# Mixer with a mixture of experts: 2 MB weight loads with 16 KB rows, and modulation on the tensor engine

## The chip, the cores and the metric

The kernel runs on one core of a Trainium2 chip, in FP32. The metric is the device time of one launch in microseconds (us). Three runs of the kernel before took 1287.95 to 1289.67 us, median 1289.12. The trace comes from one further, profiled execution of 1286.36 us. TensorE (PE) multiplies matrices, VectorE (DVE), ScalarE (ACT) and GpSimd (POOL) do the rest, and SyncE (SP) issues most of the loads. Each engine works through its own instructions in a fixed order.

## The reference

256 latent tokens and 256 context tokens of width 1024 go through one layer:

```python
sh1, sc1, g1, sh2, sc2, g2 = adaln(c, w_ada[l], b_ada[l])        # silu(c) @ w_ada + b_ada, 6 x 1024
csh1, csc1, cg1, csh2, csc2, cg2 = adaln(c_ctx, w_ada[l], b_ada[l])
pl = split_cols(modulate(rms_norm(x, norm1_g[l]), sh1, sc1) @ w_in[l])
pc = split_cols(modulate(rms_norm(ctx, norm1_g[l]), csh1, csc1) @ w_in[l])
yc_ml, yl_ml = mlstm_mixer(pc[:4], pl[:4], ...)                  # 4 heads, both directions
yc_hg, yl_hg = hgrn2_mixer(pc[4:], pl[4:], ...)                  # 4 heads, both directions
x = x + g1 * (jnp.concatenate([yl_ml, yl_hg], axis=-1) @ w_out[l])
hl2 = modulate(rms_norm(x, norm2_g[l]), sh2, sc2).reshape(bsz * seq, d)
x = x + g2 * moe_ffn(hl2, ...)                                   # top 4 of 32 experts, clamped SwiGLU
return rms_norm(x, final_g)
```

Only the first two of the six modulation vectors are wanted for the context. An expert has w_gu of 1024 x 2048 and w_down of 1024 x 1024, 12 MB; the 32 of them are 384 MB, w_in is 1024 x 4112 (all but the 16 gate columns is 16 MB), w_ada 24 MB, w_out 4 MB.

## The kernel before

**Weights.** Every large weight comes through one buffer, a ring of slots of 1 MB (8 KB in each of 128 partitions), filled by `load_rows` (L109 to L116) from SyncE's queue, in program order; a load is issued when its slot is free. The ring starts with 5 slots (`NR`) and grows by 8, 2 and 3 as the front's buffers are given up: 18 from the start of the experts on. A load of w_gu takes 128 rows of the matrix, one whole row of 8 KB to a partition. A load of w_down takes 256 rows, two rows of 4 KB to a partition, which are 128 rows apart. A load of w_in is a block of 256 columns (1 KB rows), one of w_ada or w_out 256 rows of 1024 columns.

**Splitting.** FP32 passes on TensorE are replaced in the front by fp32r passes on split numbers: `halves` (L82 to L89) makes wh, a rounded copy, on ScalarE (L87) and the rest wl on VectorE (L88). A product is then three passes (hh wh, hl wh, hh wl: L273 to L275, L290 to L292).

**The front.** The tokens come in (`xin`), are normalised and transposed into `hT`. The first 2048 columns of the modulation are 8 loads of w_ada, split, and 64 matmuls with the 4 columns of `silr` (L239, L240). Their sums `arow` are folded into columns by 16 tiny matmuls (L248), from which `mod` and `gain` come. Then `hm` = hT gain + mod, its rounded part `hh` (L325) and rest `hl` (L326) follow block by block. The gate projection takes 24 passes (L352 to L354) with the split small weight `wg`, which ScalarE's queue has loaded and VectorE split (L226, L227). The projections, the scans of the two head groups, the output gates and the output projection follow. The other 4096 columns of modulation, g1, sc2, sh2 and g2, are made beside the projections by 32 VectorE instructions (`gemv`, L586): each adds 128 rows of w_ada times `silc` to an accumulator `aacc`. `row` (L625) sums an accumulator over the partitions with two matmuls with ones, which leave the row in all partitions at once. The places of these instructions among the others are those of a scheduler that follows program order, with `issue_after` where one must not run early.

**The experts.** For a pair of experts `dispatch` gathers up to 64 tokens each, through one-hot matmuls (L923) into XT, one block of 128 features at a time. `expert` multiplies XT by 8 slots of w_gu (L941, in two groups of 64 columns that work side by side), evacuates the sum to `gu`, transposes it in 8 blocks of 128 (L950), applies the bias `bgT` and the SwiGLU, and multiplies by 4 slots of w_down (L974). `combine` adds the outputs (L986).

Of the kernel before, what the change touches and what calls it, by code (L numbers as in the profile page):

```python
# [9 lines left out]
FT = mybir.dt.float32  # L10
# [9 lines left out]
D = 1024  # L20
# [3 lines left out]
NR, NR2, NR3, NR4 = 5, 8, 2, 3  # L24
# [4 lines left out]
def tile_hybrid_backbone(  # L29
# [52 lines left out]
    def halves(src):  # L82

        wh = split.tile([128, 1024], FR, name="wh")
        wl = split.tile([128, 1024], FR, name="wl")
        with tc.high_priority(min(ahead, tc.cur_priority)):
            act(wh, src, AF.Copy)  # L87
            dve.tensor_sub(wl, src, wh.bitcast(FT))  # L88
        return wh, wl  # L89
# [36 lines left out]
    aacc = [fo.tile([128, D], FT, name=f"aacc{i}") for i in range(3)]  # L126
# [54 lines left out]


# [36 lines left out]
    wgh = px.tile([128, 8, 128], FR, name="wgh")  # L219
    wgl = px.tile([128, 8, 128], FR, name="wgl")  # L220
    nc.gpsimd.memset(wgh.bitcast(FT), 0.0)
    nc.gpsimd.memset(wgl.bitcast(FT), 0.0)
    wg4 = wg.rearrange("p a (g h) -> p a g h", g=4)
    wgh4 = wgh.rearrange("p a (g r) -> p a g r", g=4)[:, :, :, 0:4]
    wgl4 = wgl.rearrange("p a (g r) -> p a g r", g=4)[:, :, :, 0:4]
    dve.tensor_copy(wgh4, wg4)  # L226
    dve.tensor_sub(wgl4, wg4, wgh4.bitcast(FT))  # L227


    pa = [pj.tile([128, 512], FT, name="pj") for _ in range(4)]  # L230
    for g in range(2):
        for q in range(4):
            w = wa.pop(0) if wa else load_rows(w_ada[0], 256 * q, 2, g * D, D)
            for i in range(2):
                k = 2 * q + i
                wh, wl = halves(w[:, i])
                for n in range(2):
                    s = slice(n * 512, (n + 1) * 512)
                    mm(pa[2 * g + n][0:4, :], silr[:, k], wh[:, s], start=(k == 0), stop=False)  # L239
                    mm(pa[2 * g + n][0:4, :], silr[:, k], wl[:, s], start=False, stop=(k == 7))  # L240

    arow = px.tile([4, 2048], FT, name="arow")
    for n in range(4):
        (act(arow[:, n * 512:(n + 1) * 512], pa[n][0:4, :], AF.Copy) if n % 2 else
         dve.tensor_copy(arow[:, n * 512:(n + 1) * 512], pa[n][0:4, :]))
    pt = bank()
    for b in range(16):
        mm(pt[:, 2 * b:2 * b + 2], arow[:, b * 128:(b + 1) * 128], fold4, start=True, stop=True)  # L248
    mod = fc.tile([128, 16, 2], FT, name="mod")
    dve.tensor_tensor(mod, pt[:, 0:32].rearrange("p (b w) -> p b w", w=2),  # L250
                      cols[:, col["ba"]:col["ba"] + 16].unsqueeze(2).to_broadcast([128, 16, 2]), op=OP.add)
    gain = fc.tile([128, 8, 2], FT, name="gain")
    dve.scalar_tensor_tensor(gain, mod[:, 8:16], 1.0,
# [4 lines left out]
    def proj_split(w):  # L258

        return [halves(w[:, 4 * i:4 * i + 4, :].rearrange("p a f -> p (a f)")) for i in range(2)]  # L260

    def proj_cols(c0, t0s, parts=None):

        ps = [pj.tile([128, 512], FT, name="pj") for _ in t0s]
        w = None if parts else load_rows(w_in[0], 0, 8, c0, 256)
        for i in range(2):
            wh, wl = parts[i] if parts else halves(w[:, 4 * i:4 * i + 4, :].rearrange("p a f -> p (a f)"))
            for a in range(4):
                k = 4 * i + a
                for j, t0 in enumerate(t0s):  # L270
# [4 lines left out]
                    mm(o, wl[:, s], hh[:, k, t0:], start=False, stop=(k == 7))  # L275
        return ps

    def proj_tok(c0, tiles):

        ps = [pj.tile([128, 512], FT, name="pj") for _ in range(len(tiles) // 2)]  # L280
        w = load_rows(w_in[0], 0, 8, c0, 256)
        for i in range(2):
            wh, wl = halves(w[:, 4 * i:4 * i + 4, :].rearrange("p a f -> p (a f)"))
# [36 lines left out]
    first = proj_split(load_rows(w_in[0], 0, 8, 2576, 256))  # L320
    for k in range(8):
        hm = px.tile([128, 512], FT, name="hm", bufs=2)
# [108 lines left out]
    def hgrn_inputs(hp, parts=None):  # L431
# [10 lines left out]
        if hp == 0:  # L442
            gemv(2, aacc[0], last_hl)
            gemv(4, aacc[1], last_hl)
# [184 lines left out]
    for i in range(3):  # L629
        row(i, aacc[i])  # L630
# [479 lines left out]
```

## Time and profile before

| what | value |
|---|---|
| runs (3), median | 1289.12 us (1287.95 to 1289.67) |
| profiled execution, own time | 1286.36 us |
| its span, first to last instruction | 1284.3 us |
| mean granted TensorE clock | 0.982 |
| PE busy | 1164.2 us (91%) |
| DVE busy | 478.9 us (37%) |
| ACT busy | 267.7 us (21%) |
| HBM read | 453.69 MB, 354 GB/s over the span |
| share of the chain that ended last | PE 58%, DMA 34%, DVE 4% |

A busy PE isn't PE at its peak, and a share over the whole span is an average over stages with different limits. The slices of the span and the windows show each stage. The chain of waits is followed back from the last instruction; it names what released each step. MB are 10^6 bytes in the profile's rates and volumes; sizes of loads and slots are 1,048,576 bytes to the MB.

### The profile page before, as it was taken

Reading aid. Unit: us, or ns where it says so; the run is one execution under the profiler, and the core shown is the slowest. Engines: PE = TensorE matmul, PEld = TensorE weight load, DVE = VectorE, ACT = ScalarE, POOL = GpSimd, SP = SyncE. Lnnn points to the kernel's source line nnn. Section 1 sums busy time; section 2 is a strip of 40 time slices with the busy share of each in tenths; the row PEclk is TensorE's granted clock in tenths of the full one; section 3 lists DMA queues with packets and bytes.
Section 4 is the critical chain, followed back from the end, with each engine's and each line's share of the span. In section 5 each row is a group of like instructions: output and inputs, shape, how many; then the busy total and the mean of one; then the engine's idle time right before and its main releaser. Section 6 shows DMA issues by size and latency. Waiting matters only on the chain.

```text
span 1284.3 us, 14494 instructions
## 1 busy us (share of the span) xinstructions
PE 1164.2 (91%) x5708; PEld 562.0 (44%) x5709; DVE 478.9 (37%) x983; ACT 267.7 (21%) x492; POOL 108.2 (8%) x199
## 2 busy tenths in 40 slices
PE   4899999998999999889989988998899889979895
PEld 1578998896633343343323322432243234223221
DVE  7988999687121321312112221121211121112124
ACT  5666566563110000001000100100010001000001
POOL 5000000301301010110001100110020002000001
PEclk9889999998899999999999999999999999999998
DMA  9583533349899999999999999999999999999994
GB/s 332 200 295 129 180 101 126 118 171 419 323 393 416 417 418 415 402 417 416 416 417 417 417 417 417 417 417 417 416 416 417 417 417 415 417 416 417 417 415 174
DMA packets 99738, 455.77 MB, mean 355 GB/s; under 512 B 8809, under 2 KB 25282, under 8 KB 66896
## 3 DMA queue, kind: packets, MB, share of 16 engines
q1 hardware_dynamic: 97104, 452.62, 88.1%
q0 software_dynamic: 1200, 1.56, 0.4%
q8 instruction: 47, 0.77, 0.2%
q10 hardware_dynamic: 1360, 0.60, 0.2%
q14 instruction: 27, 0.22, 0.0%
HBM read 453.69 MB, written 1.05 MB: 354 GB/s over the span
## 4 chain that ended last, share of the span: by engine, by line
PE 58%; DMA 34%; DVE 4%; ACT 2%; issue 1%; POOL 0%; ACTq 0%; SPq 0%; DVEq 0%
PE pu L941 21%; DMA w<-w_gu_dram 19%; DMA w<-w_down_dram 14%; PE pd L974 9%; PE pm L923 5%; PE pm L986 3%; PE pj L275 2%; PE pj L273 2%; PE pj L274 2%; PE pt L950 1%; DMA wg<-w_in_dram 1%; PE pj L290 1%; PE pj L292 1%; PE pj L291 1%; DVE wl L88 1%; PE m L502 1%
## 5 line engine op out<-in xcount | busy, mean ns | idle before, releaser
L941 PE MATMUL pu<-w,XT 128*64 128x512 f32 x2048 | 467.9, 598 | 33.6 <-DMA w<-w_gu_dram 33.6
L941 PEld LDWEIGHTS pu<-w,XT 128*64 128x64 f32 x2048 | 136.4, 136 | 327.7 <-issue 229.2
L974 PE MATMUL pd<-w,aT 128*64 128x512 f32 x1024 | 240.5, 604 | 13.8 <-DMA w<-w_down_dram 12.3
L957 DVE TENSOR_TENSOR gl<-pt,bgT 128x512 f32<-128x512 f32 x32 | 22.1, 692 | 328.9 <-PE pt L950 328.9
L974 PEld LDWEIGHTS pd<-w,aT 128*64 128x64 f32 x1024 | 66.1, 137 | 150.3 <-issue 104.2
L76 ACT ACTIVATE gu<-pu 128x512 f32<-128x512 f32 x48 | 26.9, 595 | 493.0 <-PE pu L941 493.0
L78 DVE COPY gu<-pu 128x512 f32<-128x512 f32 x16 | 11.1, 692 | 270.5 <-ACT gu L76 270.5
L977 DVE TENSOR_TENSOR YP<-pd,g2b 64x512 f32<-64x512 f32 x64 | 44.0, 688 | 109.8 <-PE pd L974 109.1
L923 PEld LDWEIGHTS pm<-S,h 128*128 128x128 f32 x512 | 65.4, 202 | 39.3 <-issue 34.7
L914 POOL TENSOR_SCALAR S<-islot,posm 128x64 f32<-128x64 f32 x60 | 25.2, 443 | 675.2 <-PE pm L929 606.1
L923 PE MATMUL pm<-S,h 128*128 128x128 f32 x512 | 73.9, 294 | 2.2 <-DVE S L914 1.0
L986 PE MATMUL pm<-YP,GT 128*128 128x512 f32 x128 | 62.6, 614 | 11.0 <-DVE YP L977 11.0
L88 DVE TENSOR_TENSOR wl<-w,wh 128x1024 fp32r<-128x1024 f32 x55 | 66.6, 1218 | 6.0 <-ACT wh L87 5.7
L87 ACT ACTIVATE wh<-w 128x1024 fp32r<-128x1024 f32 x55 | 57.5, 1061 | 43.8 <-PE pj L274 22.1
L925 ACT ACTIVATE XT<-pm 128x512 f32<-128x512 f32 x32 | 19.0, 596 | 203.7 <-PE pm L923 203.7
L275 PE MATMUL pj<-hh,wl 128*128 128x512 f32 (+1 forms) x160 | 58.6, 371 | 3.0 <-DVE wl L88 3.0
L274 PE MATMUL pj<-hl,wh 128*128 128x512 f32 (+1 forms) x160 | 59.6, 373 | 0.0
L273 PE MATMUL pj<-hh,wh 128*128 128x512 f32 (+1 forms) x160 | 59.0, 374 | 0.2 <-ACT wh L87 0.2
L950 PE MATMUL pt<-ident,gu 128*128 128x128 f32 x256 | 39.3, 283 | 14.9 <-ACT gu L76 14.9
L950 PEld LDWEIGHTS pt<-ident,gu 128*128 128x128 f32 x256 | 27.3, 141 | 54.3 <-ACT gu L76 32.6
L960 ACT ACTIVATE sg<-gl 128x512 f32<-128x512 f32 x32 | 20.2, 630 | 142.5 <-DVE gl L958 142.5
L986 PEld LDWEIGHTS pm<-YP,GT 128*128 128x128 f32 x128 | 21.9, 189 | 50.2 <-issue 26.3
(455 smaller groups left out, 1236.6 us busy)
## 6 DMA issues: line engine op xcount, KB each, us to landing
w<-w_gu_dram SPq DMA_DIRECT2D x256, 1024.0 KB, 19.9
w<-w_down_dram SPq DMA_DIRECT2D x128, 1024.0 KB, 20.1
w<-w_ada_dram SPq DMA_DIRECT2D x24, 1024.0 KB, 6.2
w<-w_in_dram SPq DMA_DIRECT2D x16, 1024.0 KB, 5.8
w<-w_out_dram SPq DMA_DIRECT2D x4, 1024.0 KB, 5.0
xin<-x_dram SPq DMA_DIRECT2D x1, 1024.0 KB, 7.5
xin<-ctx_dram SPq DMA_DIRECT2D x1, 1024.0 KB, 12.3
x<-x_dram POOLq DMA_DIRECT2D x1, 1024.0 KB, 5.3
```

The source lines that it names most:

```text
L76: act(o, i, AF.Copy)
L87: act(wh, src, AF.Copy)
L88: dve.tensor_sub(wl, src, wh.bitcast(FT))
L273: mm(o, wh[:, s], hh[:, k, t0:], start=(k == 0), stop=False)
L274: mm(o, wh[:, s], hl[:, k, t0:], start=False, stop=False)
L275: mm(o, wl[:, s], hh[:, k, t0:], start=False, stop=(k == 7))
L923: mm(p_[:, i * ns:(i + 1) * ns], h2[:, a, (k + i) * 128:(k + i + 1) * 128], S[:, a, 0:nj].rearrange("p j s -> p (j s)"), start=(a == 0), s ...
L941: mm(ps[64 * j:64 * j + 64, n * 512:(n + 1) * 512], XT(k), w[:, 0, j * 1024 + n * 512:j * 1024 + (n + 1) * 512], start=(k == 0), stop=(k = ...
L950: nc.tensor.transpose(pt[:, f * 128:(f + 1) * 128], s[:, f * 128:(f + 1) * 128], ident)
L974: mm(pd_[64 * n:64 * n + 64, :], aT[:, k], w[:, i, n * 512:(n + 1) * 512], start=(k == 0), stop=(k == 7))
L977: dve.tensor_mul(yp[:, f], pd_[64 * n:64 * n + 64, :], g2b[64 * n:64 * n + 64, f])
L986: mm(p_, GTs[j][0:ns, a * 128:(a + 1) * 128], YP[0:ns, j, n * 512:(n + 1) * 512], start=(j == 0), stop=(j == np_ - 1))
```

## The change

It has four parts.

1. A ring slot is 2 MB, and there are 3, then 3, 2 and 1 more: 18 MB as before. `load_rows` gives each partition whole consecutive rows, 16 KB of the matrix: two rows of w_gu or four of w_down. So a partition holds features 2m and 2m + 1, or 4m to 4m + 3, and the other operand is read to match: h2 with a step of two elements (`hv`), gu with a step of four (`sv`), the biases likewise. The last load of the last w_down is issued as four.
2. w_in comes in two blocks to a slot (`load_in`, two loads of 1 MB), w_out in two loads of 2 MB (`load_blocks`).
3. No modulation is split. `gemv` now runs FP32 matmuls whose fixed operand is `silr`, 32 columns wide (two used), in four groups of 32 columns for four blocks of 512 outputs: 32 of them for the first 2048 columns, and 64 for the rest, called by `rows` among the projections. Four transposes (`columns`) replace the folding. The rows for all partitions go through a scratch in DRAM (`scr`) and are read back with broadcast loads from GpSimd's queue.
4. The token loads are issued ahead of all weights. `hm` stays in `hT`, and the modulated blocks are made one by one, with the first two split halves of w_in in the queue between them. The gate projection runs after the first projection, as 8 FP32 matmuls of 32 columns and one that adds up the four groups (`sel4`); its weight comes on GpSimd's queue.

The core of the diff:

```diff
-NR, NR2, NR3, NR4 = 5, 8, 2, 3
+NR, NR2, NR3, NR4 = 3, 3, 2, 1
...
+    def slot():
...
+        return pools[(loaded[0] - 1) % len(pools)].tile([128, 4096], FT, name="w")
...
+    def load_rows(w, r0, n, parts=1):
+
+        v = slot().rearrange("p (a f) -> p a f", a=n)
+        src = w[r0:r0 + 128 * n, :].rearrange("(p a) f -> p a f", a=n)
+        for i in range(parts):
+            q = slice(i * n // parts, (i + 1) * n // parts)
+            nc.sync.dma_start(v[:, q], src[:, q])
+        return v
+
+    def load_in(*c0):
+
+        v = slot().rearrange("p (j a f) -> p j a f", j=2, a=8)
+        for j in range(2):
+            nc.sync.dma_start(v[:, j], w_in[0, :, c0[j]:c0[j] + 256].rearrange("(a p) f -> p a f", p=128))
+        return v[:, 0], v[:, 1]
...
+    def gemv(gp, qs):
+
+
+        pa = pj.tile([128, 512], FT, name="pj")
+        for q in qs:
+            w = load_blocks(w_ada[0], 256 * q, 2, 2 * D * gp)
             for i in range(2):
...
+                for j in range(4):
+                    mm(pa[32 * j:32 * j + 32, :], silr[:, 2 * q + i], w[:, i, j * 512:(j + 1) * 512],
+                       start=(q == qs[0] and i == 0), stop=(q == qs[-1] and i == 1))
+        return pa
...
     for k in range(8):
...
+        hm = hT[:, k]
+        with queued(act_):
+            act_.append(act(hm[:, 0:256], hm[:, 0:256], AF.Identity, bias=mod[:, k, 1:2], scale=gain[:, k, 1:2]))
...
+        for j in ([k - 1] if k else []) + ([7] if k == 7 else []):
+            if j % 4 == 0:
+                first.append(halves(quarter(wf[0], j // 4), (act_[-1], dve_[-1])))
+            with queued(act_):
+                act_.append(act(hh[:, j], hT[:, j], AF.Copy))
...
+    first = proj_cols(None, (0, 0), first)
+    pg4 = bank()
     for k in range(8):
-        mm(pg, wgh[:, k], hh[:, k], start=(k == 0), stop=False)
-        mm(pg, wgh[:, k], hl[:, k], start=False, stop=False)
-        mm(pg, wgl[:, k], hh[:, k], start=False, stop=(k == 7))
+        with tc.issue_after(last_p[0].ins):
+            mm(pg4[32 * (k % 4):32 * (k % 4) + 32, :], wgp[:, k], hT[:, k], start=(k < 4), stop=(k >= 4))
...
+    def rows(gp, half):
...
+        dve.tensor_add(t, t, gemv(gp, (2 * half, 2 * half + 1)))
+        if half:
...
+            nc.gpsimd.dma_start(scr[gp - 1].rearrange("(j f) -> j f", f=512), t[0:128:32, :])
...
+    nc.gpsimd.dma_start(g1b, bcast(scr[0, 0:D], D))
+    nc.gpsimd.dma_start(sc2, bcast(scr[1, 0:D], D))
...
+        hv = h2.rearrange("p a (q m i) -> p a q i m", q=4, i=2)
...
+            w = w if k % 2 else load_rows(wg_, k * 128, 2)
...
+        sv = s.rearrange("p (q m i) -> p q i m", q=2, i=4)
...
+            w = load_rows(wd_, q * 512, 4, parts if q else 1)
```

SyncE's queue at the start, before (weights, then tokens, in turn; the last two numbers of a shape are the rows and their length in elements):

```order
L115 DMA w<-w_ada_dram 128x2x1024
L151 DMA xin<-x_dram 128x2x1024
L115 DMA w<-w_ada_dram 128x2x1024
L153 DMA xin<-ctx_dram 128x2x1024
L115 DMA w<-w_ada_dram 128x2x1024 x6
L115 DMA w<-w_in_dram 128x8x256 x2
L115 DMA w<-w_ada_dram 128x2x1024 x8
L115 DMA w<-w_in_dram 128x8x256 x6
```

and now:

```order
L175 DMA xin<-x_dram 128x1024 x2
L175 DMA xin<-ctx_dram 128x1024 x2
L119 DMA w<-w_ada_dram 128x2x2048 x4
L135 DMA w<-w_in_dram 128x8x256 x8
L119 DMA w<-w_ada_dram 128x2x2048 x2
L135 DMA w<-w_in_dram 128x8x256 x2
L119 DMA w<-w_ada_dram 128x2x2048 x2
```

The tokens stand ahead of all weights, the first 2048 columns of w_ada are four loads, and the other loads of w_ada stand in pairs, later among those of w_in.

SyncE's queue where the expert loads begin, before:

```order
L115 DMA w<-w_out_dram 128x2x1024 x4
L115 DMA w<-w_gu_dram 128x2048 x15
L115 DMA w<-w_down_dram 128x2x1024
L115 DMA w<-w_gu_dram 128x2048
L115 DMA w<-w_down_dram 128x2x1024
L1064 TENSOR_LOAD cnt_i
```

and now:

```order
L119 DMA w<-w_out_dram 128x4x1024 x2
L128 DMA w<-w_gu_dram 128x4096 x5
L128 DMA w<-w_down_dram 128x4096
L128 DMA w<-w_gu_dram 128x4096 x3
L1098 TENSOR_LOAD cnt_i
```

Ahead of the read of the expert counts (`cnt_i`) stand 18 loads of 1 MB before and 9 of 2 MB now.

TensorE in the first scan, where the first sum over partitions stood before (L502 is the scan's, L273 to L275 a projection's, L625 that of `row`):

```order
L275 MATMUL pj<-hh,wl 128x512
L273 MATMUL pj<-hh,wh 128x512
L625 MATMUL t<-aacc_96,ones 128x512
L274 MATMUL pj<-hl,wh 128x512
L275 MATMUL pj<-hh,wl 128x512
```

and now, where the first half of `rows(1, 0)` stands (L541 is the scan's, L298 to L300 and L314 the projections'):

```order
L298 MATMUL pj<-hh,wh 128x512
L299 MATMUL pj<-hl,wh 128x512
L300 MATMUL pj<-hh,wl 128x512
L259 MATMUL pj<-w,silr 32x512 x14
L541 MATMUL m<-ql,kl 128x128 x4
L259 MATMUL pj<-w,silr 32x512 x2
L314 MATMUL pj<-wh,hh 128x256
```

The single matmuls with ones are gone from among the passes, and 16 matmuls of 32 columns stand almost in one piece; 48 more follow in later pieces.

## Rows read from the trace of the kernel before

**Rows 1.** PE, DMA and rate in 40 equal slices of the span (part 2 of the page).
```profile
PE   4899999998999999889989988998899889979895
...
DMA  9583533349899999999999999999999999999994
GB/s 332 200 295 129 180 101 126 118 171 419 323 393 416 417 418 415 402 417 416 416 417 417 417 417 417 417 417 417 416 416 417 417 417 415 417 416 417 417 415 174
```

**Rows 2.** Chain of waits in order of time: start us, us, what.
```profile
1.72 16.50 DMA wg<-w_in_dram
...
1245.72 20.26 DMA w<-w_down_dram
1266.03 1.96 PE pd L974 x8
```

**Rows 3.** Windows: us, busy PE, PEld, DVE, ACT, POOL, clock, DMA share, GB/s.
```profile
645.00:665.00 20.00, 18.41 (x86) 5.79 (x82) 5.41 (x9) 1.23 (x2) 0.00 (x0) 1.00 1.02 422
697.00:705.00 8.00, 8.00 (x42) 3.12 (x38) 0.00 (x0) 0.87 (x2) 3.22 (x7) 1.00 1.02 408
982.00:1102.50 120.50, 109.62 (x504) 38.97 (x502) 23.13 (x38) 8.72 (x17) 9.23 (x16) 1.00 1.02 417
331.10:1266.00 934.90, 861.23 (x3961) 313.26 (x3960) 188.63 (x310) 70.83 (x129) 64.30 (x120) 1.00 1.01 412
```

**Rows 4.** DMA queues and DMA issues (parts 3 and 6 of the page).
```profile
q8 instruction: 47, 0.77, 0.2%
...
w<-w_gu_dram SPq DMA_DIRECT2D x256, 1024.0 KB, 19.9
```

**Rows 5.** Windows, the first 20 us.
```profile
0.00:10.00 10.00, 0.25 (x1) 0.19 (x2) 8.63 (x19) 4.52 (x7) 9.34 (x24) 1.00 0.82 293
10.00:20.00 10.00, 4.43 (x10) 1.11 (x10) 4.61 (x22) 7.46 (x11) 7.14 (x18) 1.00 1.05 387
```

**Rows 6.** TensorE timeline, first projection: start us, us, line, names, count, idle before.
```profile
51.42 0.76 PE L352 MATMUL pj<-hh,wgh 128*128 128x512 f32 x1 [2.23 <-ACT hh L325]
```

**Rows 7.** ScalarE's timeline at the first tokens.
```profile
50.66 1.13 ACT L325 ACTIVATE hh<-hm 128x512 fp32r<-128x512 f32 x2
```

**Rows 8.** Chain of waits, single matmuls: start us, us, what.
```profile
55.60 0.43 PE pj L274
...
60.45 0.23 PE pj L352
...
200.19 0.86 PE t L625 x2
...
331.21 7.02 PE pu L941 x32
```

**Rows 9.** TensorE's timeline, a stalled projection.
```profile
85.23 0.80 PE L275 MATMUL pj<-hh,wl 128*128 128x256 f32 x2 [2.98 <-DVE wl L88]
```

**Rows 10.** Windows, TensorE's clock and the loads in the front.
```profile
86.00:90.00 4.00, 4.00 (x21) 4.00 (x20) 3.96 (x7) 0.61 (x2) 0.00 (x0) 0.50 0.65 178
100.00:200.00 100.00, 100.00 (x658) 91.33 (x657) 94.62 (x191) 61.70 (x100) 0.42 (x4) 1.00 0.40 129
330.00:340.00 10.00, 10.00 (x59) 5.03 (x59) 0.00 (x0) 0.87 (x2) 3.91 (x8) 1.00 0.58 213
```

**Rows 11.** Lines from 0 to 330: busy us, mean ns of one, idle before.
```profile
L87 ACT ACTIVATE wh<-w 128x1024 fp32r<-128x1024 f32 x55 | 57.5, 1061 | 43.8 <-PE pj L274 22.1 <-PE pj L239 5.3 <-PE pj L292 5.0
L586 DVE SCALAR_TENSOR_TENSOR aacc<-w,silc,aacc 128x1024 f32<-128x1024 f32 x32 | 40.6, 1278 | 0.1
```

**Rows 12.** SyncE's queue as the expert loads begin: start us, us, issues.
```profile
267.19 43.18 SPq L115 DMA_DIRECT2D w<-w_gu_dram  x15
...
311.39 23.80 SPq L115 DMA_DIRECT2D w<-w_down_dram  x3
```

**Rows 13.** Lines from 982 to 1102.5, four experts.
```profile
L923 PE MATMUL pm<-S,h 128*128 128x128 f32 x64 | 9.2, 286 | 0.0
...
L950 PE MATMUL pt<-ident,gu 128*128 128x128 f32 x32 | 5.0, 283 | 2.3 <-ACT gu L76 2.3
```

More of the change, by code (lines that the diff above doesn't have):

```diff
@@ L80, in tile_hybrid_backbone, with halves @@
     ahead = 100
-    def halves(src):
+    def halves(src, behind=()):
         wh = split.tile([128, 1024], FR, name="wh")
         wl = split.tile([128, 1024], FR, name="wl")
-        with tc.high_priority(min(ahead, tc.cur_priority)):
+        with tc.high_priority(min(ahead, tc.cur_priority)), ExitStack() as st_:
+            for i in behind:
+                st_.enter_context(tc.issue_after(i.ins))
             act(wh, src, AF.Copy)
@@ L231, in tile_hybrid_backbone @@
-    for g in range(2):
-        for q in range(4):
-            w = wa.pop(0) if wa else load_rows(w_ada[0], 256 * q, 2, g * D, D)
-            for i in range(2):
[L235 to L248, printed above, removed]
+    sel16 = px.tile([128, 16], FT, name="sel16")
+    dve.tensor_reduce(sel16, ident.rearrange("p (j r) -> p r j", r=32)[:, 0:16], axis=AX.X, op=OP.add)
@@ L252, in tile_hybrid_backbone, with quarter @@
     gain = fc.tile([128, 8, 2], FT, name="gain")
-    dve.scalar_tensor_tensor(gain, mod[:, 8:16], 1.0,
+    gain_ = dve.scalar_tensor_tensor(gain, mod[:, 8:16], 1.0,
                              cols[:, col["g1n"]:col["g1n"] + 8].unsqueeze(2).to_broadcast([128, 8, 2]),
                              op0=OP.add, op1=OP.mult)
-    def proj_split(w):
-        return [halves(w[:, 4 * i:4 * i + 4, :].rearrange("p a f -> p (a f)")) for i in range(2)]
-    def proj_cols(c0, t0s, parts=None):
+    def quarter(w, i):
+        return w[:, 4 * i:4 * i + 4, :].rearrange("p a f -> p (a f)")
@@ L434, in hgrn_inputs @@
         hv = cp.tile([128, 4, 256], FT, name="hv", bufs=2)
-        for d_, c0 in ((0, 2576), (1, 3088)):
-            ps = proj_cols(c0 + 256 * hp, (0, 0), None if d_ else parts)
+        for d_ in range(2):
+            ps = first if first and not d_ else proj_cols(wf[d_], (0, 0))
             for i in range(2):
@@ L613, in out_gate @@
                 act(o, ps, AF.Copy)
-    h0 = hgrn_inputs(0, first)
-    scan_end = hgrn_scan(0, *h0)
-    h1 = hgrn_inputs(1)
-    g1b, sc2, sh2 = aacc[0:3]
-    def row(i, dst):
-        for n in range(2):
-            f = slice(n * 512, (n + 1) * 512)
-            p_ = bank(True)
-            mm(p_, ones, aacc[i][:, f], start=True, stop=True)
-            act(dst[:, f], p_, AF.Identity, bias=one_c) if i == 1 else act(dst[:, f], p_, AF.Copy)
-    gemv(3, aacc[2], scan_end)
-    for i in range(3):
-        row(i, aacc[i])
+    h0 = hgrn_inputs(0, wf, first)
+    hgrn_scan(0, *h0)
+    h1 = hgrn_inputs(1, load_in(2832, 3344))
+    rows(1, 0)
     mlstm_v()
-    scan_end = hgrn_scan(1, *h1)
+    rows(1, 1)
+    hgrn_scan(1, *h1)
     mlstm_qk()
+    rows(2, 0)
     fs.close()
@@ L817, in tile_hybrid_backbone @@
     out_gate(3600, 512, True)
+    rows(2, 1)
     for a in range(2):
```

208 lines of the change are left out of this document (104 added, 104 removed).

## The prediction

> **What bounds the kernel now.** I read the slices first [rows 1]: TensorE is full for about the first quarter of the span while the DMA engines idle for more than half of it, and from the tenth slice on the DMA row stands at 9 with 417 GB/s in nearly every slice. Then the chain of waits [rows 2]: its first long piece is a small load, wg, 16.50 us, and its last pieces are expert loads one behind the other, with 8 matmuls behind the last one. So two stages: a front that TensorE bounds, and an expert stream that the loads bound. The windows [rows 3] say how firmly: over four experts in the steady part (120.5 us) DMA share is 1.02 at 417 GB/s, and PE is busy 109.62 us of it.
>
> The front ends when the first expert matmul runs, at 331.2 [rows 8]. The issue queue [rows 12] shows that the buffer for weights, 18 slots of 1 MB, was by then given out whole: 15 loads of w_gu from 267.19 on, two more, and the eighteenth at 311.39. From 330 to 340 the DMA share falls to 0.58 [rows 10], since no slot is free. The buffer stays at 18 MB. So a front that is shorter by some us moves all that follows by as much: the stream can't run further ahead.
>
> **The sum** is made against the profiled execution, 1286.4 us (1284.3 of span and 2.1 around it), 2.8 below the median of 1289.1; I add 2.8 at the end.
>
> *A. The rate of the expert stream.* The windows split by row length [rows 3]: where loads of 8 KB rows (w_gu) are in flight, 422 GB/s; where those of 4 KB rows (w_down), 408. One MB is 65,536 bytes for each of 16 engines: 2.485 us at 422 and 2.570 at 408, for 8 and 16 rows an engine. The 8 rows more cost 0.085 us, 10.7 ns each (10 to 11 within the rounding). At 16 KB there are 4 rows an engine, four fewer than at 8 KB: 2.485 − 0.043 = 2.442 us, 429.4 GB/s. That is an extrapolation, so bounds: no gain beyond 8 KB gives 422; rows that cost nothing at all give 2.485 − 0.085 = 2.400, 437. There is also a row of packets that were 16 KB long: instruction loads, 47 packets, 0.77 MB, 0.2% of 16 engines' span [rows 4], that is 41 us / 47 = 0.87 us for one where the extrapolation has 0.61. They were moved beside other traffic, and the 0.2% is one digit, so I give that row little weight; it is why a rate no better than now stays possible. From 331.1 to 1266.0, 384 MB less the 18 already loaded are moved: 366 × 1.0486 = 383.8 million bytes, 920 us at 417 of the 934.9. At 429.4: 893.8. **−26.6** (−10.9 at 422, −42 at 437; above zero by the last row).
>
> The Trainium skill, "DMA: Bandwidth & Descriptors", section "Why small descriptors are slow (HBM only)", puts a packet's fixed cost at about 3 cycles; with the 850 MHz of its section "Where 436 GB/s comes from" that is 3.5 ns (an estimate from that page) against the 10.7 of the rows. It speaks against the change: by it 16 KB rows would reach 424 GB/s, A would be −16 and the time 1265; the measured step decides, for it is this stream's own.
>
> *B. The start.* Now, first projection at 51.42 [rows 6]. Ahead of it the first modulation matmuls waited on split weights made by ACT and DVE, and DVE itself on wg. Afterwards nothing is split there: 10.49 million bytes (2 MB of tokens, 8 MB of w_ada) must land. 2.93 land by 10.0 at 293 GB/s, the other 7.56 at 387 GB/s, the next row's rate, by 29.5 [rows 5]. Then 1.0 until the load is seen (0.5 to 2, no row separates it), 2.0 for the 8 matmuls of the last load (0.25 each, under E), 0.6 for a copy (as hh's 0.57 [rows 7]), 1.0 for four transposes (0.28 each [rows 13]), 0.4 allowed for two small sums, and on ACT two blocks of hm and one of hh, at 0.57, with one half of the weights between them (1.06 [rows 11]), 2.7 together: 37.2. **−14.2**. If TensorE takes 32-column matmuls two at a time (0.439, under E) and slowly, as 0.43 stands to 0.23 in [rows 8], the 32 of them take 28 us from about 14 on, beside 32 transposes, and B is −3; one at a time, +20 or more.
>
> *C. The gate projection*: 24 passes of 0.23 [rows 8] go, 5.5; eight 32-column matmuls at 0.25 and one full FP32 matmul of 0.86 come, 2.9. **−2.6**.
>
> *D.* At 85.23 TensorE had waited 2.98 us for a split half that DVE makes [rows 9], and from 86 to 90 its granted clock is 0.50, the lower of its levels (1.2 GHz) [rows 10]. DVE now has 32 products of 1278 ns fewer in the front [rows 11]. I take **−2** (0, if another split half is late there, to −6).
>
> *E. 4096 columns of modulation move from DVE to TensorE.* DVE's 40.6 us lay beside a TensorE that is busy 100.00 of 100 us [rows 10], so taking them away gives nothing; what TensorE gets is all on the path: 64 FP32 matmuls of 32 columns. Not one stands in the trace. A full one is 0.86 [rows 8]; those of 64 columns in two halves of the array are 7.02 us for 16, 0.439, so two run at once. Four at once: 0.22 each, 14 us; only two at once: 28; one at a time: 55. I take 0.25, near the first, for the halving is measured for two and the code makes all four quarters independent: +16. Four transposes more, +0.9. Eight matmuls with ones, 0.86 each [rows 8], go: −6.9. **+10.0** (8 to 22). The loads stay beside a queue with share 0.40; four broadcasts of 0.5 MB more fit in the idle 4 us from 330 to 340, and fewer bytes are wanted before. If a broadcast queued like an expert load, it would be late by up to 19.9 us [rows 4]; that end is in the third rival.
>
> *F. Coarser slots.* The first slot is free after two k-tiles, 16 matmul instructions of 0.22, instead of one [rows 8]: **+1.7** once. *G.* The last load comes in four pieces, so that 4 and not 8 instructions (1.96 [rows 2]) follow the last piece: **−1.0**. The second load of w_out now waits for a slot until the last quarter of the first is used, with fewer expert loads issued meanwhile; the idle 4 us hide that.
>
> Sum: −26.6 −14.2 −2.6 −2 +10.0 +1.7 −1.0 = −34.7. 1286.4 − 34.7 + 2.8 = **1254.5**.
>
> **Rivals.** *First: rows of 16 KB run as those of 8 KB.* For: the two windows give one step, not a curve, and the instruction packets are slow. Against: nothing between 4 and 8 KB hints at an end. Then A is −10.9 and the time 1270.
>
> *Second: the 32-column matmuls run only two at once.* For: two is all that the trace shows. Against: 0.439 is the half of 0.86 within 2%, with no sign of a limit. E costs 12 more and B 11: 1278.
>
> *Third: the front waits for weights.* It has three slots of 2 MB where it had five of 1 MB, and some 14 loads; a wait of 2 us at each (2 MB at 387 GB/s is 5.4 us, of which a fresh slot hides some) is +28: 1282. Against: DMA share is 0.40, and a 2 MB slot holds two projections' weights.
>
> *Fourth, on the other side: TensorE becomes the bound of the expert stage.* h2 is read with a step of two elements and gu with a step of four. If that doubles both groups (9.2 and 5.0 us in four experts [rows 13]), PE needs 123.8 of them against 117.0 for the faster loads. It decides from +7.4, and from +12 the kernel is slower than before. 934.9 / 120.5 = 7.76 such stretches: 7.76 × (123.8 − 117.0) = +53, time 1307. Against: 286 ns for 128 columns is no longer than 283 for the transposes, so reads don't set it now; nothing shows strided ones.
>
> The Trainium skill, "SBUF — State Buffer", section "Door 1: The DMA port swizzle (why `[64,N]` ≈ `[32,N]`)", says that a 16-byte line must be hit twice for full speed. A step of four FP32 hits each line once, a step of two twice; by that rule only gu's 5.0 would grow, to 114.6, still hidden. No run here shows it.
>
> **How the numbers follow.** Forecast 0.52; first rival 0.17, second 0.12, third 0.08, fourth 0.05; and 0.06 for better than 1238 (rows that cost nothing). The forecast's own range is 1245 to 1264. The range of 1238 to 1281 leaves out the 0.06, the fourth and most of the third. About 0.2% is what a measurement here tells from no change, 1286.5 to 1291.7: slower than that are the fourth and the worse part of the third, 0.08; within it 0.04, from the third and from the second and first together; faster 0.88.
>
> **What would show it.** A: steady DMA share above 1 at 427 to 432 GB/s, the two levels of 422 and 408 gone, four experts in 117 us. B: the first projection near 37. E: the windows of the 64 new matmuls at 0.22 to 0.27 each, and TensorE still full from 100 to 260. F and G: expert matmuls from about 322, and 4 behind the last load. I am wrong if the steady rate is still near 417, if the first expert matmul is not earlier than 331, or if the idle time ahead of expert matmuls is no longer put down to loads.

## The result and the profile after

Four runs of the changed kernel took 1248.18 to 1249.74 us, median 1248.71, beside 1288.53 for four of the kernel before: ratio 0.9693 (95% interval 0.9677 to 0.9710). The forecast was 1254.5 in a range of 1238 to 1281. The profiled execution took 1248.19, its span 1246.4, so 37.9 of span have gone.

The slices of the changed kernel (part 2 of the page):

```profile
PE   4899999998999999989999987998899789879985
...
DMA  9723556639799999999999999999999999999993
GB/s 372 240 73 131 202 199 235 241 124 428 326 429 426 427 427 426 415 427 427 426 427 427 428 426 429 426 427 428 427 426 426 428 428 427 427 426 427 428 427 158
```

Beside [rows 1], the steady slices of the DMA rate stand at 426 to 429 GB/s instead of 415 to 418, but for one in each (415 and 402), and the front is shorter by less than a slice. TensorE's row looks alike.

The chain of waits: start us, us, what.

```profile
316.62 13.88 PE pu L973 x64
...
1172.87 39.13 DMA w<-w_down_dram
...
1222.08 7.11 PE pd L1007 x32
```

The first expert matmul starts at 316.62 (331.21 in [rows 8]), the last down product ends at 1229.2 (1268.0 in [rows 2]). So 14.6 us come from the front and 936.8 − 912.6 = 24.2 from the expert stage; the last steps after it take 0.9 longer.

Two windows of the expert stage (us; busy PE, PEld, DVE, ACT, POOL; clock; DMA share; GB/s). The first is four experts from one like place to the next:

```profile
768.20:887.20 119.00, 106.79 (x502) 41.72 (x503) 22.86 (x38) 8.83 (x16) 7.84 (x16) 1.00 1.01 427
316.60:1229.00 912.40, 843.62 (x3969) 330.45 (x3968) 187.57 (x310) 71.38 (x129) 60.33 (x120) 1.00 1.00 422
```

Four experts take 119.0 and not 120.5 in this stretch, at 427 GB/s [rows 3]; the forecast had 117, and their 50.3 million bytes alone are 117.9 us at 427. PE is busy 106.79 of it, so the loads still bound the stage. In the twelve windows of 10 us from 650 to 770 the rate lies between 422 and 431; no level near 408 is left.

TensorE's timeline in the front: the last load's modulation matmuls, the first projection, then the first and the last pass of the third projection.

```profile
30.26 2.55 PE L259 MATMUL pj<-w,silr 128*32 128x512 f32 x16 [2.79 <-DMA w<-w_ada_dram]
...
37.71 1.22 PE L298 MATMUL pj<-hh,wh 128*128 128x512 f32 x2 [3.09 <-ACT hh L361]
...
64.72 0.28 PE L298 MATMUL pj<-hh,wh 128*128 128x256 f32 x1
...
70.34 0.28 PE L300 MATMUL pj<-hh,wl 128*128 128x256 f32 x1
```

The first projection comes at 37.71 instead of 51.42 [rows 6]. The third projection, in which TensorE had stalled at 85.23 and run at the lower clock [rows 9, 10], lasts from 64.72 to its last pass at 70.34.

Checkpoints of both traces, start of each unless it says end:

| step | before | after | difference |
|---|---|---|---|
| first projection | 51.42 | 37.71 | −13.7 |
| third projection, first pass | 81.51 | 64.72 | −16.8 |
| third projection, last pass | 94.29 | 70.34 | −23.9 |
| output projection, last product | 308.68 | 289.70 | −19.0 |
| first expert matmul | 331.21 | 316.62 | −14.6 |
| last down product, end | 1268.0 | 1229.2 | −38.8 |

### The profile page after: what moved, and what is told of

Same layout as the page of the kernel before. It is cut to its first block, busy times and chain, and to the rows that moved or that the text cites. A ratio compares the mean times of both kernels' runs of the same rounds, so it can differ in the third digit from the quotient of the medians.

```text
span 1246.4 us, 14117 instructions
## 1 busy us (share of the span) xinstructions
PE 1136.3 (91%) x5790; PEld 566.7 (45%) x5791; DVE 423.2 (34%) x935; ACT 250.0 (20%) x469; POOL 102.3 (8%) x199
## 4 chain that ended last, share of the span: by engine, by line
PE 57%; DMA 37%; DVE 3%; ACT 1%; issue 1%; SPq 0%; POOL 0%; DVEq 0%; ACTq 0%
DMA w<-w_down_dram 21%; PE pu L973 19%; DMA w<-w_gu_dram 15%; PE pd L1007 7%; PE pm L955 4%; PE pm L1019 4%; PE pj L299 3%; PE pj L298 2%; PE pj L300 2%; DMA w<-w_ada_dram 2%; PE pj L259 2%; PE pt L983 1%; PE pj L316 1%; PE pj L314 1%; PE pj L315 1%; PE m L759 1%
## 5 line engine op out<-in xcount | busy, mean ns | idle before, releaser
L973 PE MATMUL pu<-w,XT 128*64 128x512 f32 x2048 | 456.4, 595 | 33.6 <-DMA w<-w_gu_dram 33.5
L973 PEld LDWEIGHTS pu<-w,XT 128*64 128x64 f32 x2048 | 142.7, 137 | 324.7 <-issue 270.3
L1007 PE MATMUL pd<-w,aT 128*64 128x512 f32 x1024 | 231.4, 597 | 17.6 <-DMA w<-w_down_dram 15.7
L1007 PEld LDWEIGHTS pd<-w,aT 128*64 128x64 f32 x1024 | 70.0, 137 | 153.8 <-issue 126.6
L945 POOL TENSOR_SCALAR S<-islot,posm 128x64 f32<-128x64 f32 x60 | 25.9, 454 | 662.0 <-PE pm L955 473.1
L955 PEld LDWEIGHTS pm<-S,h 128*128 128x128 f32 x512 | 65.1, 201 | 17.4 <-issue 16.0
L955 PE MATMUL pm<-S,h 128*128 128x128 f32 x512 | 68.7, 290 | 2.2 <-DVE S L945 1.0
L298 PE MATMUL pj<-hh,wh 128*128 128x512 f32 (+1 forms) x160 | 57.7, 368 | 3.1 <-ACT hh L361 3.1
L300 PE MATMUL pj<-hh,wl 128*128 128x512 f32 (+1 forms) x160 | 57.3, 362 | 0.0
L90 DVE TENSOR_TENSOR wl<-w,wh 128x1024 fp32r<-128x1024 f32 x39 | 47.5, 1222 | 28.0 <-ACT wh L89 27.8
L983 PEld LDWEIGHTS pt<-ident,gu 128*128 128x128 f32 x256 | 33.7, 210 | 35.6 <-ACT gu L76 19.7
L983 PE MATMUL pt<-ident,gu 128*128 128x128 f32 x256 | 40.3, 298 | 9.1 <-ACT gu L76 9.1
L89 ACT ACTIVATE wh<-w 128x1024 fp32r<-128x1024 f32 x39 | 41.0, 1060 | 26.6 <-PE pj L299 20.1
```

The lines of the kernel that those rows point to most:

```text
L298: mm(o, wh[:, s], hh[:, k, t0:], start=(k == 0), stop=False)
L300: last_p[0] = mm(o, wl[:, s], hh[:, k, t0:], start=False, stop=(k == 7))
L955: mm(p_[:, i * ns:(i + 1) * ns], hv[:, a, (k + i) // 2, i % 2], S[:, a, 0:nj].rearrange("p j s -> p (j s)"), start=(a == 0), stop=(a == 1))
L973: mm(ps[64 * j:64 * j + 64, n * 512:(n + 1) * 512], XT(k), w[:, k % 2, j * 1024 + n * 512:j * 1024 + (n + 1) * 512], start=(k == 0), stop= ...
L983: nc.tensor.transpose(pt[:, f * 128:(f + 1) * 128], sv[:, f // 4, f % 4], ident)
L1007: mm(pd_[64 * n:64 * n + 64, :], aT[:, k], w[:, i, n * 512:(n + 1) * 512], start=(k == 0), stop=(k == 7))
```

## The experiments

All are edits of the changed kernel except one, which edits the kernel before. A time is a median, a ratio stands to the kernel before on the same chip. "First expert" and "stage" are from each run's trace: the start of the first expert matmul in TensorE's timeline (the chain of waits, in the lines shown below, has it up to 0.1 later), and from there to the end of the last down product.

| run | us | ratio (95%) | first expert | stage |
|---|---|---|---|---|
| changed kernel | 1248.71 | 0.9693 (0.9677 to 0.9710) | 316.6 | 912.6 |
| 1. rows of 8 and 4 KB | 1271.26 | 0.9870 (0.9848 to 0.9891) | 316.8 | 935.6 |
| 2. rows of 8 KB | 1262.23 | 0.9799 (0.9779 to 0.9818) | 317.4 | 926.3 |
| 3. expert part alone | 1267.14 | 0.9849 (0.9829 to 0.9869) | 337.4 | 912.6 |
| 4. later modulation twice | 1265.73 | 0.9837 (0.9818 to 0.9856) | 333.8 | 912.8 |
| 5. later modulation on VectorE | 1280.42 | 0.9943 (0.9923 to 0.9963) | 347.5 | 912.8 |
| 6. the same, half of it early | 1275.95 | 0.9930 (0.9913 to 0.9946) | 343.8 | 912.7 |
| 7. VectorE's order | 1248.22 | 0.9688 (0.9667 to 0.9709) | 316.4 | 913.2 |
| 8. TensorE kept busy | 1248.74 | 0.9707 (0.9689 to 0.9724) | 316.5 | 912.6 |
| 9. ScalarE's order too | 1244.73 | 0.9659 (0.9645 to 0.9672) | 313.1 | 912.7 |
| 10. last activation earlier | 1249.95 | 0.9711 (0.9695 to 0.9728) | 318.3 | 913.0 |
| 11. last load in one piece | 1250.60 | 0.9725 (0.9709 to 0.9741) | 318.1 | 913.8 |

Runs 10 and 11 don't touch the front, and still have the first expert at 318.3 and 318.1: a difference of 1.7 us there can come without any edit to it.

### The row's length (1 to 3)

**1.** The loads stay at 2 MB, only the rows are as before:

```diff
-        src = w[r0:r0 + 128 * n, :].rearrange("(p a) f -> p a f", a=n)
+        src = w[r0:r0 + 128 * n, :].rearrange("(a p) f -> p a f", p=128)
-        hv = h2.rearrange("p a (q m i) -> p a q i m", q=4, i=2)
+        hv = h2.rearrange("p a (q i m) -> p a q i m", q=4, i=2)
-        sv = s.rearrange("p (q m i) -> p q i m", q=2, i=4)
+        sv = s.rearrange("p (q i m) -> p q i m", q=2, i=4)
...
```

> The changed kernel with its 2 MB loads and slots, but w_gu in rows of 8 KB and w_down in rows of 4 KB as before, and all reads without a step. Theory (the row's length sets the rate): steady rate back to 417 GB/s from 427, 383.8 MB take 920 us and not 899, so +21.6 on 1248.7: about 1270; the four transposed blocks' weight loads fall back from 0.21 to 0.14 us. Rival (the larger load or its coarser slots set the rate): 427 GB/s stays, 1249.

The window from 700 to 1100:

```profile
700.00:1100.00 400.00, 350.57 (x1645) 132.15 (x1643) 78.12 (x130) 28.81 (x52) 23.41 (x48) 1.00 1.02 417
```

417 GB/s, to the digit of before, and the stage is 1.2 short of before's 936.8. So the load's size and the coarser slots bring nothing of note; the row's length brings the gain.

**2.** w_down comes as two pairs of rows to a partition, so that every row is 8 KB:

```diff
...
+            src = w[r0:r0 + 512, :].rearrange("(h p b) f -> p h b f", h=2, b=2)
...
```

> The changed kernel with 8 KB rows for both w_gu and w_down, 2 MB loads. Theory (a fixed cost per packet, so half of the step is left between 8 and 16 KB): 422 GB/s, 909.5 us for 383.8 MB instead of 898.8, so about 1259. Rival (rows beyond 8 KB bring nothing; all came from w_down leaving 4 KB): 427 GB/s and 1249.

```profile
700.00:1100.00 400.00, 355.77 (x1662) 135.81 (x1660) 75.88 (x126) 28.18 (x51) 23.41 (x48) 1.00 1.01 421
```

421 GB/s. The three stages give the price of a packet twice; a packet here is one row, as it goes to one partition. An expert's 12 MB are 128, 96 and 48 packets for each engine (rows of 8 and 4, of 8, and of 16 KB), and 366 MB are 30.5 experts. From 1 to 2: (935.6 − 926.3) / (32 × 30.5) = 9.5 ns. From 2 to the changed kernel: (926.3 − 912.6) / (48 × 30.5) = 9.4 ns. The runs with the changed kernel's loads have stages from 912.6 to 913.2 (11 aside, whose last load differs), so the two prices are known to some 0.5 ns and agree. One fixed cost per packet holds from 4 to 16 KB; the rival that nothing is gained beyond 8 KB falls by 13.7 us.

**3.** The kernel before with the expert part alone changed; its front keeps split modulation and 1 MB loads, in halves of 2 MB slots:

```diff
...
-            w = load_rows(wg_, k * 128, 1, 0, 2048)
+            w = w if k % 2 else load_big(wg_, k * 128, 2)
...
-            w = load_rows(wd_, q * 256, 2, 0, 1024)
...
+            w = load_big(wd_, q * 512, 4, parts if q else 1)
...
```

> The kernel before with the expert part alone changed: 2 MB loads of 16 KB rows, 9 slots of 2 MB, the reads with a step; the front with its split modulation, its products on VectorE and five half slots. Theory (the stream's gain of 24 us and the front's of 14 add up): 1288 - 24 = 1264. Rival (part of the stream's gain hangs on the earlier front, or the front's loads on the slots): 1270 or more.

```profile
337.42 13.88 PE pu L964 x64
```

The stage takes 912.6, as in the changed kernel, from a start 21 us later. The gain of the stream doesn't hang on the front. The time is 3 above the theory's because this front is 6.2 late against before; that its slots are freed in pairs is the likely cause, and wasn't tried apart.

### Modulation (4 to 6)

**4.** Each of the 64 later matmuls has one more behind it, with zeros as the fixed operand:

```diff
...
+                for j in range(4 if gp else 0):
+                    mm(pa[32 * j:32 * j + 32, :], silz, w[:, i, j * 512:(j + 1) * 512],
...
```

> The changed kernel with each of the 64 later 32-column matmuls followed by one more of the same size whose fixed operand is zero. Theory (TensorE is full there, and four run side by side at 0.223 each in the trace): +14.3, about 1263. If only two ran side by side in truth, +28: 1277. Rival (they lie beside other work): 1249.

```profile
333.81 13.88 PE pu L979 x64
```

The first expert comes 17.2 later: 64 × 0.269. In the changed kernel's own chain, 28 instructions, that is 14 matmuls, take 3.56 us:

```profile
127.78 3.56 PE pj L259 x28
```

That is 0.254 each with what the sequence costs at its ends. They lie wholly on the path, and four run side by side; two at once would be 0.44 [rows 8].

**5.** The later 4096 columns go back to VectorE, in the same places of the program:

```diff
-        dve.tensor_add(t, t, gemv(gp, (2 * half, 2 * half + 1)))
...
+        for u in range(2):
+            w = load_blocks(w_ada[0], 512 * u, 4, 2 * D * gp + D * half)
+            for i in range(4):
+                dve.scalar_tensor_tensor(acc, w[:, i], silr[:, 4 * u + i, 0:1], acc, op0=OP.mult, op1=OP.add)
+            ...
+            mm(pa[p0 + 32 * j:p0 + 32 * j + 32, :], ones[:, 0:32], acc[:, j * 512:(j + 1) * 512], start=True, stop=True)
...
```

> The changed kernel with the last 4096 columns of modulation back on VectorE (32 products of 1024 columns, 40.6 us of VectorE) and 8 short matmuls with ones instead of 64 on TensorE; their weights come as 4 KB rows, everything else stays. Theory (TensorE bounds the front, VectorE has room): 64 x 0.223 = 14.3 us go, 8 x 0.25 = 2 come, about -12: 1236. Rival (the move off VectorE is what ended the stall at 81 to 90 and the waits of the later scan, some 12 us in all, so they come back): 1247 to 1250.

Neither: it is 31 us slower at the first expert. What TensorE waited for from 52 to 345 (us in total, times, longest), and two windows of the front:

```profile
PE m L541 <- ACT ql L534: 10.0, 3, 5.2
PE m L735 <- DVE mk L340: 9.8, 1, 9.8
```

```profile
100.00:200.00 100.00, 89.21 (x583) 79.36 (x581) 94.66 (x171) 50.19 (x77) 2.83 (x7) 0.93 0.45 161
200.00:260.00 60.00, 46.51 (x287) 39.52 (x288) 50.62 (x121) 26.14 (x59) 11.92 (x16) 0.81 0.47 168
```

TensorE has lost its full row (89.21 of 100, 46.51 of 60, granted clock 0.93 and 0.81) to waits for the scan's steps on ScalarE and VectorE. VectorE is busy 94.66 of 100, but it was busy 94.62 in the kernel before, beside a TensorE that was full [rows 10]; so the share alone doesn't tell why. That the products now stand in VectorE's queue ahead of steps that TensorE waits for is the likely cause, and isn't shown by this run alone.

**6.** The same, with the first two of the four parts ahead of the third projection, where the first products stood before:

```diff
+        if hp == 0:
+            rows(1, 0)
+            rows(1, 1)
         wq, wv = load_in(1552 + 256 * hp, 2064 + 256 * hp)
...
```

> As the kernel with the last 4096 columns of modulation on VectorE, but the first half of them stands in program order where the kernel before had its first products, ahead of the third projection. There the first expert matmul came at 347.5 instead of 316.6. Theory (it was the place among the scan's steps, on VectorE's queue, that cost 31, and TensorE's 17 are still saved): the first expert matmul near 316 or earlier, 1250 or less. Rival (VectorE has no room for 40 us anywhere in the faster front, so what TensorE is spared is paid there): half or more of the 31 stays, 1264 or more.

```profile
PE pj L635 <- DVE tn L584: 18.9, 1, 18.9
PE pj L635 <- DVE acc L631: 6.2, 1, 6.2
```

27 of the 31 us stay, so the time is the rival's. But here TensorE waited with its short matmuls with ones (L635) for the products, 25 us in two waits (the trace names tn, a step of the scan between the products in VectorE's queue; the last product ends at 85.25 and the matmul starts at 85.40), where the kernel before had its first sum far later, at 200.19 [rows 8]. These two places don't prove that no place exists. A version with the products early and the sums late wasn't tried, so the rival's reason, that VectorE has no room, isn't shown.

### The end of the front (7 to 9)

Of the 19.0 us that the output projection is earlier, 4.4 are lost before the first expert. VectorE's queue there (L803 first step of the gated residual, L804 second, L805 third; start us, us):

```profile
290.75 0.69 DVE L803 TENSOR_TENSOR h<-pj,row 128x512 f32<-128x512 f32 x1 [3.25 <-PE pj L802]
291.61 0.69 DVE L803 TENSOR_TENSOR h<-pj,row 128x512 f32<-128x512 f32 x1 [0.17 <-PE pj L802]
292.22 2.49 DVE L804 TENSOR_TENSOR x<-x,h 128x512 f32<-128x512 f32 x4
294.62 1.89 DVE L805 TENSOR_TENSOR h<-x,row 128x512 f32<-128x512 f32 x3
```

and TensorE's:

```profile
289.70 1.88 PE L802 MATMUL pj<-w,hT 128*128 128x512 f32 x4
291.41 0.63 PE L906 MATMUL t<-ident,bgs 128*128 128x128 f32 x4
295.37 1.97 PE L813 MATMUL m<-ident,h 128*128 128x128 f32 x8 [3.32 <-DVE h L805]
```

All four first steps stand ahead of the second steps. So the first 128 tokens wait for the projection of the second 128, and TensorE for 3.32 us; the clock is then at the lower level (window of the front's end, below the one of its middle):

```profile
100.00:200.00 100.00, 99.46 (x711) 83.95 (x712) 84.06 (x179) 59.09 (x98) 1.95 (x6) 1.00 0.43 153
295.00:298.00 3.00, 2.63 (x12) 2.34 (x12) 3.00 (x16) 1.80 (x4) 0.00 (x0) 0.50 1.01 431
```

**7.** VectorE finishes the first 128 tokens first:

```diff
...
-            dve.tensor_mul(h2[:, a, f], po_[a][n], g1b[:, f])
+            with tc.issue_after((last_h[0] or last_e[0]).ins):
+                dve.tensor_mul(h2[:, a, f], po_[a][n], g1b[:, f])
...
```

> The changed kernel with one order changed: VectorE finishes the gated residual of the first 128 tokens (three steps for each half) ahead of the second 128's first step, instead of all four first steps, all four second, all four third. Theory (TensorE's wait of 3.3 us at 292 and its low clock until 306 come from that queue, and the front's end moves the whole stream): -4, about 1244.5. Rival (the full buffer or the loads of experts set the end of that stage, so nothing moves): 1248.7.

No gain. ScalarE's queue (L910 is the copy of the expert biases, L809 the squares) and VectorE's show why:

```profile
291.81 1.10 ACT L910 ACTIVATE bgT<-t 128x512 f32<-128x512 f32 x1 [5.37 <-PE t L909]
292.69 0.70 ACT L809 ACTIVATE pj<-x 128x512 f32<-128x512 f32 x1
```

```profile
290.48 0.69 DVE L806 TENSOR_TENSOR h<-pj,row 128x512 f32<-128x512 f32 x1 [0.34 <-PE pj L804]
294.63 0.16 DVE L818 TENSOR_TENSOR ss<-ss 128x1 f32<-128x1 f32 x1 [3.46 <-ACT pj L809]
```

The sum of squares at 294.63 waited 3.46 us for ScalarE's squares. Their input was ready at 289.41, but they stood behind the copy of the biases, which itself had waited 5.37 us for TensorE. So the time is the rival's, but not for its reason, as 9 shows.

**8.** To this, unused matmuls where TensorE is idle, two in each router stage and three meant for the wait before the first projection:

```diff
...
+        for _ in range(2):
+            mm(fd, ident, g1b[:, 0:512], start=True, stop=True)
...
```

> The changed kernel with the order of the gated residual as in the run before it, and unused FP32 matmuls where TensorE is idle: three before the first projection, two in each router stage. Theory (idle TensorE falls to its lower clock, 0.50 granted, and the next 8 passes and the router's 32 matmuls pay for it): 1.7 at the first projection and 2 to 3 at the router back, about 1244.5. Rival (VectorE's chain of small steps sets both ends, and the clock doesn't matter): 1248.

```profile
295.00:298.00 3.00, 1.64 (x12) 1.32 (x12) 3.00 (x10) 1.33 (x4) 0.00 (x0) 0.97 1.00 426
301.00:304.00 3.00, 3.00 (x4) 1.35 (x5) 2.96 (x9) 0.80 (x2) 3.00 (x3) 0.50 0.97 415
```

With the first pair the clock was 0.97 from 295 to 298, where run 7 had 0.51; the second pair was queued behind a wait of its own and ran at 0.50, and the three earlier ones ran at 17.56, long before the wait. The first projection came 1.0 earlier, at 36.67, yet nothing of it was left at the first expert (316.5). Nothing is gained with the clock up in part of the stage; for the rest this run decides nothing.

**9.** As 7, with the four squares ahead of ScalarE's copies that wait for TensorE, and the bias copy behind them:

```diff
...
+            with tc.issue_after(last_sq[0].ins):
+                act(hT2[:, a, k:k + 4], p_.rearrange("p (i t) -> p i t", i=4), AF.Copy)
...
```

> The changed kernel with the order of the gated residual as in the run with VectorE's order changed, and on ScalarE the two squares of each 128 tokens ahead of the copies that wait for TensorE, the copy of the expert biases behind all four squares. There VectorE waited 3.46 us at 294.6 for a square that stood behind the bias copy on ScalarE. Theory (the end of the front is set by ScalarE's and VectorE's queues, in the order in which they hold the second layer norm's steps): the first expert matmul 3 to 4 us earlier than at 316.5, 1245. Rival (the selection of experts, a chain of small steps on VectorE, takes as long from wherever it starts, and its start hangs on the second half's projection): 316, 1248.

VectorE in the same place, and the first expert:

```profile
291.19 0.15 DVE L819 TENSOR_TENSOR ss<-ss 128x1 f32<-128x1 f32 x1
```

```profile
313.16 13.88 PE pu L978 x64
```

The sum of squares stands at 291.19, unwaited, and the first expert at 313.16, 3.5 earlier. The theory held. That TensorE's clock stayed up longer here would be another cause; the windows of this run and, below, of 7 speak against it:

```profile
295.00:300.00 5.00, 2.90 (x25) 2.56 (x23) 5.00 (x27) 2.15 (x4) 3.89 (x3) 0.86 1.00 421
295.00:300.00 5.00, 4.24 (x19) 3.38 (x19) 5.00 (x25) 2.44 (x7) 0.50 (x1) 0.50 1.05 442
```

The granted clock is 0.86 here and 0.50 there, but from the sum of squares to the first expert it takes 21.9 here and 21.8 there (VectorE is busy all of both windows). The whole gain lies ahead of that sum. The time of 1244.73 us is the best of all; its interval (0.9645 to 0.9672) lies just below the changed kernel's (0.9677 to 0.9710).

### The last expert (10, 11)

**10.** The last activation ahead of the down product before it:

```diff
+        if e == NE - 1:
+            next(jobs[e])
         if e > 0:
             next(jobs[e - 1])
...
```

> The changed kernel, but the last expert's activation stands ahead of the down product of the one before. Theory (after the last load of w_gu TensorE does half a down product, 3.65 us, ahead of the transposes on which the last expert's chain hangs, so the four last small loads aren't the end): -1.5 to -3, about 1246.5. Rival (the last loads' landing, near 1227 in the trace, sets the end): 1248.7.

The stage is 913.0 beside 912.6: no gain, as the rival has it.

**11.** The last load in one piece:

```diff
-                         4 if e == NE - 1 else 1)
+                         1)
```

> The changed kernel with the last load of the last w_down issued in one piece of 2 MB. Theory (in the trace the last down product doesn't wait for its loads but for VectorE, so the four pieces bring nothing): 1248.7. Rival (they spare up to 8 to 12 matmul instructions behind the last landing, as forecast): +1 to +3.5, 1250 to 1252.

TensorE's last down product is cut in two by a wait:

```profile
1223.61 3.65 PE L1007 MATMUL pd<-w,aT 128*64 128x512 f32 x16 [1.49 <-DVE YP L1010]
1228.23 3.65 PE L1007 MATMUL pd<-w,aT 128*64 128x512 f32 x16 [0.97 <-DMA w<-w_down_dram]
```

The wait is 0.97 and the stage 1.2 longer. So my reading of the unwaited product was wrong: it doesn't wait because the pieces land in time.

## Why the prediction was right, point by point

**A, the stream: −26.6 forecast, with F and G −25.9; −24.2 measured.** The mechanism is shown by 1 and 2: rows alone, a fixed cost per packet, linear to 16 KB. Its size was off: two windows with rates rounded to 1 GB/s gave 10.7 ns (the rounding leaves 9.9 to 11.4, more than the 10 to 11 that I wrote), three whole stages give 9.4 to 9.5. The steady rate is 427, not 429.4. The row of instruction packets (0.87 us for 16 KB) would have said that nothing is won; it was rightly given little weight, for at 427 GB/s over 16 engines a row of 16 KB takes 0.61. Of the Trainium skill, "DMA: Bandwidth & Descriptors", section "Why small descriptors are slow (HBM only)", the cost of about 3 cycles is 3.5 ns (an estimate with that page's clock); these runs show 9.4, so here the page has less than half of it.

**B, the start: −14.2 forecast, −13.7 measured.** The last modulation load was consumed from 30.26, near the forecast's landing. The first passes then ran at the lower clock (granted 0.53 from 37 to 42). How much of it came from each of the edits there, the tokens ahead, the weights unsplit and wg moved, wasn't tried apart.

**C, the gate: −2.6 forecast.** Its 8 matmuls now take 1.85 us as 16 instructions:

```profile
55.06 1.85 PE m L391 x16
```

At the third projection the gain has grown from 13.7 to 16.8, by 3.1, in which C lies.

**D, the stall: −2 forecast, within 0 to −6; −7.2 by the checkpoints** (12.8 us for the third projection before, 5.6 now). 1.4 of this is no stall: the kernel before did four passes of the next projection and three small matmuls from 90.52 to 91.92, which the changed kernel does later.

```profile
90.52 0.47 PE L273 MATMUL pj<-hh,wh 128*128 128x512 f32 x1
```

So the stall brought about 5.8, near the end of the range. I saw a wait of 2.98 and some us of low clock, and kept back most of it in case another split half were late. VectorE's queue in the kernel before shows that the half (L88) stood behind modulation's products (L586) and steps of the gate. The products are on TensorE now and that gate step (L392 here) comes at 85.77, after the third projection, so the wait and the low clock went whole:

```profile
82.05 1.27 DVE L586 SCALAR_TENSOR_TENSOR aacc<-w,silc,aacc 128x1024 f32<-128x1024 f32 x1
83.24 0.67 DVE L392 TENSOR_REDUCE umax<-WW 36x4 f32<-36x512 f32 x1
...
83.97 1.20 DVE L88 TENSOR_TENSOR wl<-w,wh 128x1024 fp32r<-128x1024 f32 x1
```

**E, the later modulation: +10.0 forecast.** The price on TensorE was right (0.25 taken; 0.254 in the chain, 0.269 by 4), and the second rival, two at once, is out. From the third projection's end to the output projection the front lost 4.9 (23.9 to 19.0), or 3.5 for like work, without the 1.4 of D. E's terms there, 16 + 0.9 − 6 × 0.86, ask for 11.7. The 8.2 between them are in rows that I hadn't costed. 32 matmuls of 64 rows stand in another order, and take 3.4 less; the first row is of the kernel before, the second of the changed one:

```profile
L695 PE MATMUL m<-mq,mk 64*128 64x256 f32 x32 | 9.3, 405 | 0.0
```

```profile
L725 PE MATMUL m<-mq,mk 64*128 64x256 f32 x32 | 5.9, 408 | 0.0
```

Two waits of TensorE at the output projection in the kernel before, 2.9 in all, are gone:

```profile
PE pj L754 <- DVE yTl L747: 1.9, 1, 1.9
PE pj L752 <- ACT yTh L746: 1.0, 1, 1.0
```

With the wait of 1.9 went the lower clock behind it: from 296.32 to 302.39 the kernel before ran 14 passes at 0.43 and not 0.23 each (granted 0.50 from 296 to 300), some 2.8 us more (an estimate from these rows); the changed kernel's clock is 1.00 from 278 to 290. The three sums (3.4, 2.9 and 2.8) make 9.1, a little more than the 8.2. No run took them one by one.

What 5 and 6 say against me is the sentence that taking the products off VectorE gives nothing. D is one price of them, and put back into the faster front they cost 27 to 31 us. How much of that a better place would save is open.

**F and G.** The four pieces of the last load spare about 1 us, as forecast (11). F wasn't measured apart; run 1, which has both and rows as before, has a stage 1.2 shorter than the kernel before, where F and G gave +0.7.

**What was missed.** Of the eight matmuls with ones, two stood at the end of the front, where I had taken 1.7 as a gain; 4.4 were lost there. Most of it is the order in which the queues of VectorE and ScalarE now hold the residual's steps: 9 gives 3.5 of it back, and keeping TensorE busier gave nothing. In the kernel before, VectorE had done all the steps of the first 128 tokens by 308.2, ahead of the second 128's first step at 309.74. The other 0.9 is open.

**The rivals.** The first is out by 2, the second by 4. The third didn't come: from 100 to 200 PE is busy 99.46 of 100. The fourth didn't come, for the loads still end last, but its half that the Trainium skill foretold is there. In "SBUF — State Buffer", section "Door 1: The DMA port swizzle (why `[64,N]` ≈ `[32,N]`)", a 16-byte line wants two hits. Weight loads of four experts in the changed kernel, h2 with a step of two (L955) and gu with a step of four (L983):

```profile
L955 PEld LDWEIGHTS pm<-S,h 128*128 128x128 f32 x64 | 7.9, 196 | 2.1 <-issue 2.1
...
L983 PEld LDWEIGHTS pt<-ident,gu 128*128 128x128 f32 x32 | 4.2, 210 | 4.1 <-issue 2.4 <-ACT gu L76 1.6
```

and in run 1, where neither has a step:

```profile
L955 PEld LDWEIGHTS pm<-S,h 128*128 128x128 f32 x64 | 7.5, 192 | 2.1 <-issue 2.1
...
L983 PEld LDWEIGHTS pt<-ident,gu 128*128 128x128 f32 x32 | 3.4, 141 | 4.1 <-issue 2.4 <-ACT gu L76 1.6
```

The step of four takes a weight load from 141 to 210 ns, the step of two from 192 to 196. The trace agrees with the rule. The step of four costs 0.8 us of PEld in four experts and lies under the loads.

The forecast was 5.8 us too high. Too low by 1.7 in A with F and G, 0.5 in B, 6.1 at the end of the front (4.4 lost, 1.7 counted as won) and 0.9 after the last product; too high by 0.5 in C, 3.8 in D, 8.2 in E, and 2.3 since this kernel's profiled execution lies 0.5 below its median where I had added 2.8. That makes 5.6. The stream's term was right by its mechanism; the front brought 14.6 where B to E gave 8.8, and errors of both signs lie under that, up to 8 us each. That they nearly cancel is luck.

## What to carry to other kernels

A stream that fills the DMA engines has a cost per packet beside its bytes: give a partition consecutive rows and let the other operand's access pattern take the step, and take the slope from whole stages, not from short windows. An engine that is busy 84 to 95 of 100 us beside a full one isn't free: what stands in its queue ahead of a small step can make the full engine wait, as in D, and work put back on it can cost more than the full engine is spared. After any shift, read the queues at the seam to the next stage; of three waits behind one another there, taking away TensorE's alone (7) gave nothing, and all of them (9) 3.5 us.

## What the runs showed of the hardware

On this stream of loads into 128 partitions, the cost of a packet is the same between 4 and 8 KB (9.5 ns) as between 8 and 16 KB (9.4 ns). FP32 matmuls of 32 columns in four groups of columns run at 0.254 us each for 512 columns of the moving operand, against 0.86 for a full one [rows 8]. A step of four FP32 elements makes a weight load of 128 by 128 1.49 times as long, 210 against 141 ns; a step of two does next to nothing, 196 against 192.
